# Hybrid decoder layer on one core: the first row norm stepped beside its output projection, convolution taps as single chains in one PSUM bank, the convolution norm in a bank of its own, and squares added on GpSimd

## The chip, the core and the metric

The kernel runs on one core of one Trainium2 chip, as one launch. The metric is device microseconds (us) for one execution of the program. The core has a matrix engine (TensorE, PE; its weight loads are listed apart as PEld), a vector engine (VectorE, DVE), a scalar engine (ScalarE, ACT), GpSimd (POOL), a sync engine (SyncE, SP) that issues loads, and DMA queues. Each engine works through its own list of instructions in a fixed order; an instruction waits until the work that it needs on other engines has signalled.

## The reference

One decoder layer over x of 1024 tokens by 1024 channels, in float32, cut to what matters here:

```
proj = x @ w_in + b_in                    # 1024 x 1792
q, k, v, a, gate = split(proj)            # 512, 128, 128, 512, 512
# attention group: window of 128, 8 heads of 64, 2 kv heads, a sink logit per head, relative bias
y_attn = sliding_window_gqa(q, k, v, sinks, rel_bias_table)
# convolution group
h = a * sigmoid(gate)
h = causal_depthwise_conv(h, conv_dw_w, conv_dw_b)        # 31 taps per channel
y_conv = silu(layer_norm(h, conv_ln_g, conv_ln_b))        # over the 512 channels
y = concat(rms_norm(y_attn, attn_out_gain), rms_norm(y_conv, conv_out_gain))
x = layer_norm(ALPHA * x + y @ w_out + b_out, ln1_g, ln1_b)
# feed-forward
hh = causal_depthwise_conv(x @ w_up, ffn_dw_w, ffn_dw_b)  # 3 taps, 5632 channels
g, u = split(hh)
x = layer_norm(ALPHA * x + (silu(g) * u) @ w_down, ln2_g, ln2_b)
```

## The kernel before

**Halves and products.** The 1024 tokens are worked in two halves, H = 0 and H = 1, of 512 tokens each. A 512-token row of one 128-channel group is one tile of 128 x 512. A float32 product is made as three products of fp32r parts: each operand is split into a high part (`wh`, `oh`: a cast on ACT, L231) and a low part (`wl`, `ol`: a subtraction on POOL, L233), and TensorE multiplies high by high, high by low and low by high (`mm3`, L265, L266, L268).

**Stages.** For each half there are input projections (`load_x`, `glu`, `proj_kv`, `proj_q`), the 31-tap convolution (`conv`), its norm (`conv_norm`), attention (`attn`: per 128-token block and pair of heads a `front`, scores and softmax; a `mid`, the transposes L541; a `back`, the products with v, L562 to L564; and per block a `tail`, L581), the output projection (`out_proj`: 16 tiles of 128 x 2 x 256, four quarters of the columns `q` by four token blocks `t`, each added into `acc` by two DVE instructions, L652 and L654), the first row norm (`ln1`, which also transposes the normed rows into the feed-forward's operand, L278 and L282) and the feed-forward. Six of 22 channel pairs of the feed-forward are done for half 0 alone (`ffn`, up products by `mm3`, then down products); the other 16 are done for both halves together (`joint`), by seven products in place of eight. This joint loop is the last half of the run.

**The convolution.** Of 31 taps, the first KO (4 for half 0, 5 for half 1) are done as ACT multiplications (L411) added on POOL (L415); the rest, 27 and 26 of them, are a chain of DVE instructions (L421 for the first, L425 for the others), each of which reads the running sum in PSUM and writes it again, until the last writes the result tile `cy`. POOL then adds its own sum (L430). `conv_pair` works two channel groups at a time and alternates between their two chains, each in one of the two banks with the tag C.

**The convolution norm.** The mean over the 512 channels is a product with a constant matrix of 1/512 (L445). Then `y[c] - mean` on DVE (L449), a square on ACT (L451), and for each of four token blocks the sum of squares over the 512 channels as four matmuls with one column (L456, output 128 x 1). After 1/sqrt (DVE L292, POOL L293) the four columns are made into a row by a product with a diagonal matrix (L462, L464), and the rows are scaled, gated and split (L469 to L472). The same sums of squares for the RMS norm follow (L480). All these PSUM tiles have the tag C too. A float32 matmul shows as two records in the trace.

**What sets the order.** `SCRIPT` is a string of letters; each letter advances one generator by one step: `a`/`A` attention of half 0/1, `c`/`C` convolution, `n`/`N` convolution norm, `g` and `q` the projections of half 1, `o`/`O` output projection of half 0/1, `l`/`L` first row norm, `f` feed-forward of half 0. In the kernel before, `c` and `C` run their generator to its end at once. That gives the order in which the instructions are written. The framework's scheduler then sets the final order on each engine by a timeline of its own, under the data dependencies, the PSUM tiles that must come free, and two chains of order that the kernel adds: `chain` keeps the bulk products (`mm3`, the output projection of half 0, the joint products) in the order written, and `tap` does the same for the convolution's DVE taps, over both halves. DMA loads keep their order as well.

**PSUM.** Eight banks are dealt out by tag: `PS` gives A 2, S 2, T 1, Y 1, C 2. `PT` says which tags a stage cycles through: the row norm of half 0 (`ln0`) uses A, that of half 1 (`ln1`) T and C, the joint products A, T, S, A, C, S, Y, C.

Of the kernel before, what the change touches and what calls it, by code (L numbers as in the profile page):

```python
# [15 lines left out]
P = 128  # L16
S = 1024
# [16 lines left out]
LINE = 384  # L34
GROUP = 2
ALONE = 6
SCRIPT = ('0hx00j0hxixxiiiacaaaaaaaaaaaaannnaaagaggqqgaaaqkqoAAAoAAAAAo'
          'ACAoAAllAANAAAANAlAlfNfAOOOfsOsssffLLLLffff')
SKEW = (1, 2, 5)
KOFF = (4, 5)  # L40
AHEAD = 1
LNM = (0, 0, 1, 1)
XM = (1, 1)
PT = {'x0': 'AT', 'x1': 'AS', 'glu0': 'AS', 'glu1': 'A', 'kv0': 'A', 'kv1': 'A', 'q0': 'A', 'q1': 'A', 'v0': 'T', 'v1': 'T',
      'joint': 'ATSACSYC',
      'tail': 'T', 'out0': 'A', 'out1': 'A', 'ln0': 'A', 'ln1': 'TC', 'sum1': 'T', 'up0': 'A', 'up1': 'AY', 'down0': 'SY', 'down1': 'S'}
PS = {'A': 2, 'S': 2, 'T': 1, 'Y': 1, 'C': 2}
UNIT = 512
BASE = 384
D0 = 74  # L50
# [19 lines left out]
def hybrid_layer_kernel(  # L70
# [153 lines left out]
    def cdw(k, c):  # L224
        return pcol(1, k * 4 + c)
# [175 lines left out]
            nc.gpsimd.tensor_tensor(out=ql[:, i, :], in0=qf, in1=f(qh[:, i, :]), op=ALU.subtract)  # L401
            yield

    def conv_pair(H, c0, dst):
        KO = KOFF[H]
        extra = {}
        for i, c in enumerate((c0, c0 + 1)):
            for k in range(KO):
                slot = 2 * i if k == 0 else 1
                prod = at(64 * 4 * UNIT + 4 * (HC + slot * HALF), [P, HALF], F32, "cp")  # L410
                nc.scalar.mul(out=prod, in_=hconv[H, c][:, k:k + HALF], mul=cdw(k, c))  # L411
                if k == 0:
                    extra[c] = prod
                else:
                    nc.gpsimd.tensor_tensor(out=extra[c], in0=extra[c], in1=prod, op=ALU.add)  # L415
        chains = {c: psB(tag="C") for c in (c0, c0 + 1)}
        for k in range(KW - 1, KO - 1, -1):
            for c in (c0, c0 + 1):
                src = hconv[H, c][:, k:k + HALF]
                if k == KW - 1:  # L420
                    tap(nc.vector.tensor_scalar(out=chains[c], in0=src, scalar1=cdw(k, c), scalar2=cdb[c],  # L421
                                                op0=ALU.mult, op1=ALU.add))
                else:
                    to = dst[c] if k == KO else chains[c]
                    tap(nc.vector.scalar_tensor_tensor(out=to, in0=src, scalar=cdw(k, c), in1=chains[c],  # L425
                                                       op0=ALU.mult, op1=ALU.add))
            if k % 8 == 0:
                yield
        for c in (c0, c0 + 1):
            nc.gpsimd.tensor_tensor(out=dst[c], in0=dst[c], in1=extra[c], op=ALU.add)  # L430

    def conv(H):
        y = [sbt([P, HALF], "cy") for c in range(4)]
        for c0 in (0, 2):
            yield from conv_pair(H, c0, y)
        cyt[H] = y

    def conv_norm(H):
        y = cyt[H]
        mean = psB(tag="C")  # L440
        sums = [sbt([P, HALF], "nsum") for _ in range(2)]
        for i in range(2):
            nc.gpsimd.tensor_tensor(out=sums[i], in0=y[2 * i], in1=y[2 * i + 1], op=ALU.add)
        nc.gpsimd.tensor_tensor(out=sums[0], in0=sums[0], in1=sums[1], op=ALU.add)
        nc.tensor.matmul(out=mean, lhsT=ones, rhs=sums[0], start=True, stop=True)  # L445
        var = psB((P, 4), "C")
        sqs = []
        for c in range(4):
            nc.vector.tensor_tensor(out=y[c], in0=y[c], in1=mean, op=ALU.subtract)  # L449
            sq = sbt([P, HALF], "nsq")  # L450
            nc.scalar.square(out=sq, in_=y[c])  # L451
            sqs.append(sq)
        yield
        for t in range(TB):
            for c in range(4):
                nc.tensor.matmul(out=var[:, t:t + 1], lhsT=sqs[c][:, t * P:(t + 1) * P], rhs=ones[:, 0:1],  # L456
                                 start=c == 0, stop=c == 3)
        rstd = ring("crstd", 4, 2)
        rsqrt_eps(rstd, var, 4, "nrv")
        dg = sbt([P, TB, P], "nz")  # L460
        for t in range(TB):
            nc.vector.tensor_scalar(out=dg[:, t, :], in0=ident, scalar1=rstd[:, t:t + 1], scalar2=None, op0=ALU.mult)  # L462
        rb = psB(tag="C")
        nc.tensor.matmul(out=rb, lhsT=ones1, rhs=dg, start=True, stop=True)  # L464
        yield
        yh, yl = [[a[:, c, :] for c in range(4)] for a in pair(1)]
        sqs = []
        for c in range(4):
            nc.vector.tensor_tensor(out=y[c], in0=y[c], in1=rb, op=ALU.mult)  # L469
            nc.scalar.activation(out=y[c], in_=y[c], func=AF.Silu, bias=clb[c], scale=clg[c])  # L470
            nc.scalar.mul(out=yh[c], in_=y[c], mul=gain[4 + c])
            nc.vector.scalar_tensor_tensor(out=yl[c], in0=y[c], scalar=gain[4 + c], in1=f(yh[c]),  # L472
                                           op0=ALU.mult, op1=ALU.subtract)
            sq = sbt([P, HALF], "nsq")
            nc.scalar.square(out=sq, in_=y[c])
            sqs.append(sq)
        ms = psB((P, 4), "C")
        for t in range(TB):
            for c in range(4):
                nc.tensor.matmul(out=ms[:, t:t + 1], lhsT=sqs[c][:, t * P:(t + 1) * P], rhs=ones[:, 0:1],  # L480
                                 start=c == 0, stop=c == 3)
        s = ring("sC", 4, 2)
        rsqrt_eps(s, ms, 4, "nrv")
        yC[H] = (yh, yl)
        sC[H] = s
        yield

    def attn(H):
# [59 lines left out]
        def back(u):  # L548
# [16 lines left out]
            if (g, pr) == (1, 1):  # L565
                yh, yl = [a[:, :, t * P:(t + 1) * P] for a in qT[H]]
                yv = yp[t].rearrange("p (i q) -> p i q", q=P)
                for i in range(4):
                    nc.scalar.mul(out=yh[:, i], in_=yv[:, i], mul=gain[i])
                for i in range(4):  # L570
                    nc.vector.scalar_tensor_tensor(out=yl[:, i], in0=yv[:, i], scalar=gain[i], in1=f(yh[:, i]),
                                                   op0=ALU.mult, op1=ALU.subtract)
                sq = sbt([P, HALF], "sq")
                nc.scalar.square(out=sq, in_=yp[t])
                sqs[t] = sq
                yA[b] = (yh, yl)

        def tail(t):
            ms = psk("tail", (P, 4))
            for i in range(4):  # L580
                nc.tensor.matmul(out=ms[:, 0:1], lhsT=sqs[t][:, i * P:(i + 1) * P], rhs=ones[:, 0:1],  # L581
                                 start=i == 0, stop=i == 3)
            rsqrt_eps(s[:, t:t + 1], ms[:, 0:1], 1)

        n = len(units)
# [425 lines left out]
    drain(load_x(0))  # L1011
    parameters()
    for k in SCRIPT:
        if k in 'cC':
            drain(steps[k])
        else:
            next(steps[k], None)
# [60 lines left out]
```

## Time and profile before

| what | value |
|---|---|
| median of 3 runs | 1140.39 us (1139.77 to 1141.25) |
| the profiled execution | 1140.95 us, of which the span in the trace is 1139.2 us |
| busy in the span | PE 95%, PEld 79%, DVE 68%, ACT 46%, POOL 53% |
| mean granted clock of TensorE | 0.967 |
| projections of both halves begun, 0 to 120 us | PE busy 111.1 of 120 |
| attention and conv norm of half 0, projections of half 1, 120 to 233 us | PE busy 113.0 of 113, clock 0.92 |
| output projection of half 0 beside conv and attention of half 1, 233 to 317 us | DVE busy 81.1 of 84 |
| row norm of half 0, conv norm and attention of half 1, 317 to 364 us | PE busy 37.2 of 47, clock 0.75 |
| feed-forward of half 0 begun, 364 to 399 us | PE busy 34.7 of 35, clock 0.84 |
| output projection and row norm of half 1, feed-forward of half 0, 399 to 547 us | PE busy 138.7 of 148 |
| joint loop, end, 547 to 1139.2 us | PE busy 574.4 of 592.2 |

How to read the lines that follow: a row of the timeline gives start and length in us, the engine, the line of the kernel, the instruction, its output and inputs, and how many instructions were merged into the row ("x22"); in brackets stands the idle time of the engine before it and what ended it. A group row gives busy time in us and the mean length in ns, then the idle time before the group. The granted clock (PEclk) is the share of full speed that TensorE was given; 0.50 is half speed. Instructions of one engine overlap a little, so the step from one start to the next is the better price of a row of equal instructions than the length of each.

### The profile page before, as it was taken

To read this page: it belongs to the slowest core of one execution; us is meant where nothing else is said; L and a number is where in the kernel's file an instruction comes from. 1 tells how busy PE (TensorE), PEld (TensorE's weight loads), DVE (VectorE), ACT (ScalarE), POOL (GpSimd) and SP (SyncE) were. 2 spreads that over 40 slices of the span, in tenths; PEclk is the share of its full clock that TensorE was granted. 3 is DMA by queue.
4 is the path that set the end of the run, shared out by engine and by line. 5 is a ranking of instruction groups with operands and counts; after the bars stand their busy time and mean duration, and the time that the engine had idled before them with its cause. 6 is when DMAs were issued, how large, how long until landed. Compare 5 with 4: busy or idle time off the path is not lost.

```text
span 1139.2 us, 14637 instructions
## 1 busy us (share of the span) xinstructions
PE 1084.8 (95%) x5257; PEld 903.9 (79%) x5257; DVE 776.6 (68%) x1414; ACT 521.3 (46%) x1031; POOL 599.1 (53%) x468
## 2 busy tenths in 40 slices
PE   7999999998888999989999999999999999999997
PEld 5877788888876899867778787878878787888875
DVE  3699555999996355998565747474656656559656
ACT  4536897673659432444424334251524242442530
POOL 4739645446461165834837465564636373835561
PEclk9999988999968899999999999999999999999998
DMA  5534212233220034113211112121212021223421
GB/s 179 167 97 116 72 32 66 83 93 119 67 93 19 1 121 120 57 38 92 73 38 56 56 38 75 37 75 37 65 28 75 19 75 37 70 99 115 125 93 74
DMA packets 115642, 85.21 MB, mean 75 GB/s; under 512 B 20354, under 2 KB 108017, under 8 KB 115569
## 3 DMA queue, kind: packets, MB, share of 16 engines
q1 hardware_dynamic: 112368, 78.92, 23.2%
q10 hardware_dynamic: 3201, 5.35, 1.3%
q8 instruction: 41, 0.67, 0.2%
q14 instruction: 32, 0.26, 0.1%
HBM read 80.05 MB, written 4.21 MB: 74 GB/s over the span
## 4 chain that ended last, share of the span: by engine, by line
PE 45%; DVE 5%; ACT 1%; DMA 0%; POOL 0%; issue 0%; POOLq 0%; ACTq 0%
PE psC L800 2%; PE psC L798 2%; PE psC L797 2%; PE psS L800 2%; PE psS L797 2%; PE psS L798 2%; PE psA L800 2%; PE psA L798 2%; PE psA L797 2%; PE psS L717 2%; PE psS L718 2%; PE psS L719 2%; PE psA L717 1%; PE psC L717 1%; PE psA L718 1%; PE psA L719 1%
## 5 line engine op out<-in xcount | busy, mean ns | idle before, releaser
L233 POOL TENSOR_TENSOR wl<-raw,wh 128x512 fp32r<-128x512 f32 x196 | 263.0, 1354 | 223.4 <-PE psA L268 86.3
L231 ACT CAST wh<-raw 128x512 fp32r<-128x512 f32 x196 | 118.7, 619 | 172.0 <-PE psA L266 19.2
L233 POOL TENSOR_TENSOR wl<-ts,wh 128x512 fp32r<-128x512 f32 x64 | 82.5, 1296 | 149.6 <-ACT wh L231 136.5
L265 PE MATMUL psA<-x,wh 128*128 128x512 f32 x336 | 138.2, 411 | 7.9 <-DVE z L682 3.5
L266 PE MATMUL psA<-x,wh 128*128 128x512 f32 x336 | 137.4, 409 | 0.0
L425 DVE SCALAR_TENSOR_TENSOR psC<-hconv,const,psC 128x512 f32<-128x512 f32 x196 | 135.8, 742 | 0.0
L231 ACT CAST wh<-ts 128x512 fp32r<-128x512 f32 x64 | 39.4, 622 | 174.4 <-PE psS L719 31.0
L268 PE MATMUL psA<-x,wl 128*128 128x512 f32 x336 | 90.6, 404 | 0.6 <-POOL wl L233 0.6
L265 PEld LDWEIGHTS psA<-x,wh 128*128 128x128 f32 x336 | 66.1, 197 | 24.0 <-issue 4.4
L266 PEld LDWEIGHTS psA<-x,wh 128*128 128x128 f32 x336 | 66.0, 197 | 14.6 <-issue 0.7
L268 PEld LDWEIGHTS psA<-x,wl 128*128 128x128 f32 x336 | 63.9, 193 | 15.8 <-issue 1.2
L293 POOL TENSOR_TENSOR tiny<-tiny,const 128x1 f32<-128x1 f32 (+1 forms) x28 | 27.6, 989 | 61.3 <-DVE tiny L292 61.3
L233 POOL TENSOR_TENSOR ol<-or,oh 128x512 fp32r<-128x512 f32 x32 | 41.0, 1307 | 26.8 <-PE psY L564 15.4
L724 DVE TENSOR_TENSOR acc<-psS,acc 128x512 f32<-128x512 f32 x52 | 35.6, 687 | 26.9 <-PE psS L719 26.9
L797 PE MATMUL psS<-x,wh 128*128 128x512 f32 x112 | 43.6, 389 | 0.0
L797 PE MATMUL psA<-x,wh 128*128 128x512 f32 x112 | 43.6, 389 | 0.0
L798 PE MATMUL psA<-x,wh 128*128 128x512 f32 x112 | 43.6, 389 | 0.0
L798 PE MATMUL psS<-x,wh 128*128 128x512 f32 x112 | 43.6, 389 | 0.0
L797 PE MATMUL psC<-x,wh 128*128 128x512 f32 x112 | 43.6, 389 | 0.0
L798 PE MATMUL psC<-x,wh 128*128 128x512 f32 x112 | 43.6, 389 | 0.0
L415 POOL TENSOR_TENSOR cp<-cp,cp 128x512 f32<-128x512 f32 x28 | 36.0, 1286 | 13.0 <-ACT cp L411 13.0
L836 POOL TENSOR_TENSOR ts<-raw,ts 128x512 f32<-128x512 f32 x32 | 41.6, 1299 | 1.2
(340 smaller groups left out, 3084.3 us busy)
## 6 DMA issues: line engine op xcount, KB each, us to landing
raw<-in_w_up SPq DMA_DIRECT2D x56, 512.0 KB
raw<-in_w_down SPq DMA_DIRECT2D x28, 512.0 KB
raw<-in_w_in SPq DMA_DIRECT2D x20, 512.0 KB
raw<-in_x SPq DMA_DIRECT2D x8, 512.0 KB
raw<-in_w_in SPq DMA_DIRECT2D x16, 256.0 KB
acc<-in_x SPq DMA_DIRECT2D x8, 512.0 KB
or<-in_w_out SPq DMA_DIRECT2D x64, 64.0 KB
or<-in_w_out SPq DMA_DIRECT2D x8, 512.0 KB
```

Of the source, the lines that this page charges most:

```text
L231: nc.scalar.copy(out=h, in_=part)
L233: nc.gpsimd.tensor_tensor(out=l, in0=part, in1=f(h), op=ALU.subtract)
L265: m.append(nc.tensor.matmul(out=o, lhsT=wh[kt], rhs=xh[kt], start=kt == 0, stop=False))
L266: m.append(nc.tensor.matmul(out=o, lhsT=wh[kt], rhs=xl[kt], start=False, stop=False))
L268: m.append(nc.tensor.matmul(out=o, lhsT=wl[kt], rhs=xh[kt], start=False, stop=kt == KT - 1))
L415: nc.gpsimd.tensor_tensor(out=extra[c], in0=extra[c], in1=prod, op=ALU.add)
L425: tap(nc.vector.scalar_tensor_tensor(out=to, in0=src, scalar=cdw(k, c), in1=chains[c], op0=ALU.mult, op1=ALU.add))
L717: m.append(nc.tensor.matmul(out=o, lhsT=gh[:, tsl], rhs=wh, start=j == 0, stop=False))
L797: m.append(nc.tensor.matmul(out=o, lhsT=wh[k], rhs=xh[k], start=k == 0, stop=False))
L798: m.append(nc.tensor.matmul(out=o, lhsT=wh[k], rhs=xl[k], start=False, stop=False))
L800: m.append(nc.tensor.matmul(out=o, lhsT=wl[k], rhs=xh[k], start=False, stop=k == 3))
L836: nc.gpsimd.tensor_tensor(out=t, in0=x0, in1=x1, op=ALU.subtract)
```

## The change

`SCRIPT` steps the convolution of half 1 one channel group at a time, between steps of the output projection and attention, and puts four steps of the row norm of half 0 (`l`) right after the last step of its output projection. `conv_pair` becomes `conv_group`: one channel group is one chain of 27 or 26 taps, in the only bank C. The bank that this frees gets a tag of its own, N, for all tiles of `conv_norm`; the joint products use N where they had their second C, and the row norm of half 1 cycles through T, C and N. `token_sums` adds the four tiles of squares into one on POOL (three additions of 128 x 512) and then needs one matmul with one column for each token block in place of four. In attention's `tail` the squares, 512 wide, are folded by POOL to 256 and to 128, and one matmul takes the place of four.

```
-SCRIPT = ('0hx00j0hxixxiiiacaaaaaaaaaaaaannnaaagaggqqgaaaqkqoAAAoAAAAAo'
-          'ACAoAAllAANAAAANAlAlfNfAOOOfsOsssffLLLLffff')
+SCRIPT = ('0hx00j0hxixxiiiacaaaaaaaaaaaaannnaaagaggqqgaaaqkqoAAAoAAAAA'
+          'oACCCCAoAllllAANAAAANAAfNfAAOOOfsOsssffLLLLffff')
...
-      'joint': 'ATSACSYC',
-      'tail': 'T', 'out0': 'A', 'out1': 'A', 'ln0': 'A', 'ln1': 'TC', 'sum1': 'T', ...
-PS = {'A': 2, 'S': 2, 'T': 1, 'Y': 1, 'C': 2}
+      'joint': 'ATSACSYN',
+      'tail': 'T', 'out0': 'A', 'out1': 'A', 'ln0': 'A', 'ln1': 'TCN', 'sum1': 'T', ...
+PS = {'A': 2, 'S': 2, 'T': 1, 'Y': 1, 'C': 1, 'N': 1}
...
+    def conv_group(H, c, dst):
+        KO = KOFF[H]
+        for k in range(KO):
...
+        total = psB(tag="C")
         for k in range(KW - 1, KO - 1, -1):
+            src = hconv[H, c][:, k:k + HALF]
+            if k == KW - 1:
+                tap(nc.vector.tensor_scalar(out=total, in0=src, scalar1=cdw(k, c), scalar2=cdb[c],
+                                            op0=ALU.mult, op1=ALU.add))
+            else:
+                tap(nc.vector.scalar_tensor_tensor(out=dst if k == KO else total, in0=src, scalar=cdw(k, c),
+                                                   in1=total, op0=ALU.mult, op1=ALU.add))
+        nc.gpsimd.tensor_tensor(out=dst, in0=dst, in1=extra, op=ALU.add)
...
+    def token_sums(o, sqs):
+        for a, b in ((0, 1), (2, 3), (0, 2)):
+            nc.gpsimd.tensor_tensor(out=sqs[a], in0=sqs[a], in1=sqs[b], op=ALU.add)
+        for t in range(TB):
+            nc.tensor.matmul(out=o[:, t:t + 1], lhsT=sqs[0][:, t * P:(t + 1) * P], rhs=ones[:, 0:1],
+                             start=True, stop=True)
...
     def conv_norm(H):
-        mean = psB(tag="C")
+        mean = psB(tag="N")
...
-        for t in range(TB):
-            for c in range(4):
-                nc.tensor.matmul(out=var[:, t:t + 1], lhsT=sqs[c][:, t * P:(t + 1) * P], rhs=ones[:, 0:1],
-                                 start=c == 0, stop=c == 3)
+        token_sums(var, sqs)
...
+                for w in (2 * P, P):
+                    nc.gpsimd.tensor_tensor(out=sq[:, 0:w], in0=sq[:, 0:w], in1=sq[:, w:2 * w], op=ALU.add)
...
-            for i in range(4):
-                nc.tensor.matmul(out=ms[:, 0:1], lhsT=sqs[t][:, i * P:(i + 1) * P], rhs=ones[:, 0:1],
-                                 start=i == 0, stop=i == 3)
+            nc.tensor.matmul(out=ms[:, 0:1], lhsT=sqs[t][:, 0:P], rhs=ones[:, 0:1], start=True, stop=True)
...
-        if k in 'cC':
+        if k == 'c':
             drain(steps[k])
```

Three places show how the instructions move. The first is DVE around the first taps of half 1's convolution. Before, the first tap of all (L421, its source is the half's tile `hconv_1553`) stands among the last instructions of half 0's conv norm (L469 scales, L472 splits; between them two instructions of attention):

```order
L469 TENSOR_TENSOR cy_780<-cy_780,psC 128x512
L516 ISA hank_258,tiny_60<-psS,bias_577,const_61 128x256
L516 ISA tiny_60 128x1
L516 ISA hank_258,tiny_60<-psS,bias_577,const_61 128x256
L516 ISA tiny_60 128x1
L544 TENSOR_TENSOR ph_948<-psT,ph_948 128x512
L472 SCALAR_TENSOR_TENSOR x_93<-cy_777,const_61,x_92 128x512
L472 SCALAR_TENSOR_TENSOR x_93<-cy_778,const_61,x_92 128x512
L421 TENSOR_SCALAR psC<-hconv_1553,const_61 128x512
```

In the changed kernel the last tap of half 0 (to `cy_780`) is followed by the taps of half 1 (L418 and L421 now; source `hconv_1532`), which stand ahead of all instructions of half 0's conv norm:

```order
L421 SCALAR_TENSOR_TENSOR cy_780<-hconv_238,const_61,psC 128x512
L538 TENSOR_TENSOR ph_967<-psT,ph_967 128x256
L418 TENSOR_SCALAR psC<-hconv_1532,const_61 128x512
L521 TENSOR_TENSOR tiny_60<-tiny_60 128x4
L421 SCALAR_TENSOR_TENSOR psC<-hconv_1532,const_61,psC 128x512
L522 RECIPROCAL tiny_60<-tiny_60 128x4
L421 SCALAR_TENSOR_TENSOR psC<-hconv_1532,const_61,psC 128x512 x3
```

So the taps of half 1 have moved from behind the conv norm of half 0 to directly behind the last tap of half 0, and three of them in a row now belong to the same chain, each reading what the one before wrote.

The second place is PE at the conv norm of half 1, beside the transposes of half 0's row norm (L278). Before, sixteen matmuls of one column are in the list (four tiles of squares, `nsq`, for each token block); these are the last eight, with one token block's transposes between them:

```order
L456 MATMUL psC<-const_61,nsq_3165 128x1
L456 MATMUL psC<-const_61,nsq_3168 128x1
L456 MATMUL psC<-const_61,nsq_3171 128x1
L456 MATMUL psC<-const_61,nsq_3174 128x1
L456 MATMUL psC<-const_61,nsq_3165 128x1
L278 MATMUL psA<-const_61,acc_1998 128x128 x8
L456 MATMUL psC<-const_61,nsq_3168 128x1
L456 MATMUL psC<-const_61,nsq_3171 128x1
L456 MATMUL psC<-const_61,nsq_3174 128x1
```

In the changed kernel the same place has the mean (L445), the attention's tail (L576) and four matmuls of one column (L435) between the transposes of the first three token blocks:

```order
L445 MATMUL psN<-nsum_3138,const_61 128x512
L278 MATMUL psA<-const_61,acc_1976 128x128 x8
L576 MATMUL psT<-const_61,sq_1061 128x1
L278 MATMUL psA<-const_61,acc_1979 128x128 x8
L435 MATMUL psN<-const_61,nsq_3146 128x1 x4
L535 MATMUL psT<-const_61,hank_254 128x128 x4
L278 MATMUL psA<-const_61,acc_1982 128x128 x8
```

The number of such matmuls is a quarter, and transposes that stood behind them stand ahead of them.

The third place is POOL near the end of half 0's output projection. Before, the last two splits of its weights (`ol`) are followed by the additions to the convolution's last two results (L430 to `cy_2658`, `cy_2659`):

```order
L233 TENSOR_TENSOR wl_282<-raw_166,wh_284 128x512
L233 TENSOR_TENSOR wl_170<-raw_201,wh_168 128x512
L233 TENSOR_TENSOR ol_2031<-or_2027,oh_2029 128x512
L233 TENSOR_TENSOR ol_2035<-or_2027,oh_2033 128x512
L443 TENSOR_TENSOR nsum_3157<-cy_2656,cy_2657 128x512
L430 TENSOR_TENSOR cy_2658<-cy_2658,cp_781 128x512
```

In the changed kernel that addition (L423 now, to the last result `cy_2636`) stands ahead of those two splits:

```order
L423 TENSOR_TENSOR cy_2636<-cy_2636,cp_819 128x512
L233 TENSOR_TENSOR wl_282<-raw_166,wh_284 128x512
L233 TENSOR_TENSOR wl_170<-raw_201,wh_168 128x512
L233 TENSOR_TENSOR ol_2009<-or_2005,oh_2007 128x512
L233 TENSOR_TENSOR ol_2013<-or_2005,oh_2011 128x512
L570 TENSOR_TENSOR sq_1061<-sq_1061 128x256
L570 TENSOR_TENSOR sq_1061<-sq_1061 128x128
```

The last weights of the output projection are now split behind the end of the convolution, not ahead of it. The order of loads on SP is the same, load for load.

More of the change, by code (lines that the diff above doesn't have):

```diff
@@ L44 @@
 PT = {'x0': 'AT', 'x1': 'AS', 'glu0': 'AS', 'glu1': 'A', 'kv0': 'A', 'kv1': 'A', 'q0': 'A', 'q1': 'A', 'v0': 'T', 'v1': 'T',
-      'joint': 'ATSACSYC',
-      'tail': 'T', 'out0': 'A', 'out1': 'A', 'ln0': 'A', 'ln1': 'TC', 'sum1': 'T', 'up0': 'A', 'up1': 'AY', 'down0': 'SY', 'down1': 'S'}
-PS = {'A': 2, 'S': 2, 'T': 1, 'Y': 1, 'C': 2}
+      'joint': 'ATSACSYN',
+      'tail': 'T', 'out0': 'A', 'out1': 'A', 'ln0': 'A', 'ln1': 'TCN', 'sum1': 'T', 'up0': 'A', 'up1': 'AY', 'down0': 'SY', 'down1': 'S'}
+PS = {'A': 2, 'S': 2, 'T': 1, 'Y': 1, 'C': 1, 'N': 1}
 UNIT = 512
@@ L402, in proj_q @@
             yield
-    def conv_pair(H, c0, dst):
+    def conv_group(H, c, dst):
         KO = KOFF[H]
[L406 to L416, printed above, removed]
-        for k in range(KW - 1, KO - 1, -1):
[L418 to L430, printed above, removed]
@@ L432, in conv @@
-    def conv(H):
[L433 to L436, printed above, removed]
+        for k in range(KO):
+            slot = 2 * (c % 2) if k == 0 else 1
+            prod = at(64 * 4 * UNIT + 4 * (HC + slot * HALF), [P, HALF], F32, "cp")
+            nc.scalar.mul(out=prod, in_=hconv[H, c][:, k:k + HALF], mul=cdw(k, c))
+            if k == 0:
+                extra = prod
+            else:
+                nc.gpsimd.tensor_tensor(out=extra, in0=extra, in1=prod, op=ALU.add)
@@ new lines, in conv_group @@
+        total = psB(tag="C")
+        for k in range(KW - 1, KO - 1, -1):
+            src = hconv[H, c][:, k:k + HALF]
+            if k == KW - 1:
+                tap(nc.vector.tensor_scalar(out=total, in0=src, scalar1=cdw(k, c), scalar2=cdb[c],
+                                            op0=ALU.mult, op1=ALU.add))
+            else:
+                tap(nc.vector.scalar_tensor_tensor(out=dst if k == KO else total, in0=src, scalar=cdw(k, c),
+                                                   in1=total, op0=ALU.mult, op1=ALU.add))
@@ new lines, in conv_group @@
+        nc.gpsimd.tensor_tensor(out=dst, in0=dst, in1=extra, op=ALU.add)
+    def conv(H):
+        cyt[H] = [sbt([P, HALF], "cy") for c in range(4)]
+        for c in range(4):
+            conv_group(H, c, cyt[H][c])
+            yield
+    def token_sums(o, sqs):
[4 more added lines that the diff above has]
+                             start=True, stop=True)
@@ L445, in conv_norm @@
         nc.tensor.matmul(out=mean, lhsT=ones, rhs=sums[0], start=True, stop=True)
-        var = psB((P, 4), "C")
+        var = psB((P, 4), "N")
         sqs = []
@@ L462, in conv_norm @@
             nc.vector.tensor_scalar(out=dg[:, t, :], in0=ident, scalar1=rstd[:, t:t + 1], scalar2=None, op0=ALU.mult)
-        rb = psB(tag="C")
+        rb = psB(tag="N")
         nc.tensor.matmul(out=rb, lhsT=ones1, rhs=dg, start=True, stop=True)
@@ L476, in conv_norm @@
             sqs.append(sq)
[L477 to L481, printed above, removed]
+        ms = psB((P, 4), "N")
+        token_sums(ms, sqs)
         s = ring("sC", 4, 2)
```

## The prediction, made before the changed kernel was run

> **What bounds the kernel now.** I read the page's head and clock row first, then busy time by stage, then the timeline at the edges of the stages that the change touches. The page: PE is busy 95% of the span and the whole run leans on it, but its clock dips in the second quarter, where DVE is at its fullest.
>
> ```profile
> span 1139.2 us, 14637 instructions
> PE 1084.8 (95%) x5257; PEld 903.9 (79%) x5257; DVE 776.6 (68%) x1414; ACT 521.3 (46%) x1031; POOL 599.1 (53%) x468
> DVE  3699555999996355998565747474656656559656
> PEclk9999988999968899999999999999999999999998
> ```
>
> By stage (stretch; then length and the busy time with count of PE, PEld, DVE, ACT, POOL; granted clock; DMA share; GB/s):
>
> ```profile
> 120.00:233.00 113.00, 113.00 (x564) 92.85 (x562) 74.36 (x163) 88.78 (x208) 54.60 (x46) 0.92 0.23 64
> 233.00:317.00 84.00, 75.70 (x545) 70.17 (x544) 81.11 (x188) 46.88 (x133) 46.71 (x40) 0.94 0.33 101
> 317.00:364.00 47.00, 37.24 (x179) 31.03 (x178) 39.47 (x79) 33.72 (x75) 16.87 (x9) 0.75 0.14 48
> 364.00:399.00 35.00, 34.67 (x167) 29.48 (x168) 12.94 (x28) 18.74 (x42) 6.61 (x6) 0.84 0.00 0
> 547.00:1139.20 592.20, 574.37 (x2523) 472.60 (x2522) 373.26 (x615) 212.46 (x358) 315.58 (x244) 0.99 0.21 65
> ```
>
> So four stages before 399 us have different limits. Up to 233 it is PE, partly at a low clock. In the output projection of half 0 it is DVE: 81.1 of 84 us. In the row norm it is nobody's throughput: PE stands 10 of 47 us and runs at a clock of 0.75, while DVE works off the row norm, the convolution norm and attention in one list. Then PE again. The last row, more than half of the run, is PE alone; it is the same work in the changed kernel, so what is gained or lost ahead of it is passed on whole. The edges of the DVE-bound stretch are the first and the last addition of the projection, and the row norm ends where TensorE gets its operand:
>
> ```profile
> 242.75 0.45 DVE L652 SCALAR_TENSOR_TENSOR acc<-psA,tiny,acc 128x256 f32<-128x256 f32 x1
> 316.38 0.47 DVE L654 SCALAR_TENSOR_TENSOR acc<-psA,tiny,acc 128x256 f32<-128x256 f32 x1
> 356.45 0.50 PE L265 MATMUL psA<-x,wh 128*128 128x512 f32 x1 [0.88 <-DVE x L282]
> ```
>
> **Part 1: fewer matmuls of one column.** Groups (busy us, mean ns) and two runs of them:
>
> ```profile
> L456 PE MATMUL psC<-const,nsq x64: 164/352/372, 150.0 to 337.0; 128*128 128x1 f32 x64
> L480 PE MATMUL psC<-const,nsq x64: 164/250/352, 177.7 to 380.5; 128*128 128x1 f32 x64
> L581 PE MATMUL psT<-const,sq x64: 164/250/371, 185.3 to 406.7; 128*128 128x1 f32 x64
> 329.58 4.94 PE L456 MATMUL psC<-const,nsq 128*128 128x1 f32 x22 [0.35 <-ACT nsq L451]
> 377.08 2.62 PE L480 MATMUL psC<-const,nsq 128*128 128x1 f32 x20
> 150.87 0.97 PE L511 MATMUL psS<-kh,x 64*128 64x256 f32 x6
> ```
>
> 192 records (two to a matmul) become 48. A record costs 2.62 / 20 = 0.131 us at mostly full clock and 4.94 / 22 = 0.225 at the low one. Ahead of the first matmul of the output projection the written order has 40 such matmuls before and 10 now, 60 records less, 7.9 us; one more group of scores (0.97 us) has moved ahead of it. Net -6.9 us on the path, as PE is busy all of 113 us there. After the first `mm3` of the feed-forward it is again 30 matmuls less, 7.9 us by the same price, of which I count 4 (a run as long as the row norm's now stands ahead of that point, and the POOL work below must come first).
>
> **Part 2: the clock.** Rows: stretch, then PE, PEld, DVE, ACT and POOL as above, clock.
>
> ```profile
> 374.00:377.00 3.00, 3.00 (x24) 2.81 (x23) 0.95 (x4) 1.75 (x2) 1.28 (x1) 1.00 0.00 0
> 377.00:381.00 4.00, 4.00 (x30) 4.00 (x29) 2.80 (x7) 3.30 (x9) 0.55 (x1) 0.73 0.01 4
> 381.00:385.00 4.00, 4.00 (x10) 3.13 (x11) 1.02 (x3) 0.77 (x2) 1.02 (x1) 0.50 0.00 0
> 153.00:157.00 4.00, 4.00 (x24) 4.00 (x23) 2.73 (x8) 4.00 (x11) 1.35 (x2) 0.57 0.32 64
> 157.00:164.00 7.00, 7.00 (x22) 5.42 (x22) 2.56 (x10) 5.58 (x15) 2.31 (x2) 0.51 0.00 0
> ```
>
> The clock falls from 1.00 to 0.50 during and after a run of these matmuls in which PE is never idle. The stretch 120 to 233 loses 113 x 0.08 = 9.0 us to it, 364 to 399 loses 35 x 0.16 = 5.6. With runs of 8 records in place of 32, between none and all of this comes back: 0 to 14.6. I take half of the first, -4.5, and 3 of the second. The Trainium skill, "TensorE: Matmul & The Clock Gate", section "Why this matters for your kernels", ties the drop to a PE-idle gap of about 3 us. The rows above show a drop with no gap; by that rule these drops have another cause and nothing of the 7.5 comes back (rival A).
>
> **Part 3: taps as one chain.** Rows of DVE: a run of alternating taps, then a dependent pair (L808 reads the z that L806 wrote) and an independent neighbour:
>
> ```profile
> 54.88 13.91 DVE L425 SCALAR_TENSOR_TENSOR psC<-hconv,const,psC 128x512 f32<-128x512 f32 x21
> 578.25 0.74 DVE L806 SCALAR_TENSOR_TENSOR z<-psA,const,z 128x511 f32<-128x511 f32 x1
> 579.02 0.75 DVE L808 SCALAR_TENSOR_TENSOR z<-psA,const,z 128x510 f32<-128x510 f32 x1
> 579.69 0.74 DVE L806 SCALAR_TENSOR_TENSOR sq<-psC,const,sq 128x511 f32<-128x511 f32 x1
> ```
>
> A tap steps 13.91 / 21 = 0.66 us. The dependent pair steps 0.77, the independent one 0.67: +0.10, and I take 0.125 as the dearest step that I saw of this kind. No row shows a PSUM chain of taps back to back: the cost is 0 if the tap's write is ready in its own step, 0.125 by the pair. In the changed order 103 of 212 taps follow directly on a tap of their own chain, 62 in half 0 and 41 in half 1: +7.8 and +5.1 us of DVE. The first part lies where DVE is 90% busy or more (57 to 114 us) but PE is the bound; it delays half 0's conv norm, whose result is due only at the output projection, near 233 (its first addition is at 242.75). What is late next if this cover goes is the conv norm's mean, for which PE would stand. I count +1. The second part falls where DVE idles (part 4): 0.
>
> **Part 4: half 1's taps start early.** Now they stand behind the conv norm, because it holds the banks C:
>
> ```profile
> 127.00:174.00 47.00, 21.28 (x61) 0.89 0.20 49
> 174.23 0.81 DVE L421 TENSOR_SCALAR psC<-hconv,const 128x512 f32<-128x512 f32 x1
> 174.00:191.00 17.00, 7.04 (x20) 0.90 0.18 54
> 191.06 0.81 DVE L421 TENSOR_SCALAR psC<-hconv,const 128x512 f32<-128x512 f32 x1
> ```
>
> (The two stretches are of DVE alone.) DVE idles 25.7 and 10.0 us there; room for 23 taps at 0.66 + 0.125 = 18 us. In the written order 153 taps stand ahead of the first addition of the output projection before, 176 now: 23 x 0.66 = 15.2 us less in the DVE-bound stretch. Into it come the four `acc` scalings of half 1 (L627), 4 x 1.21 = 4.8:
>
> ```profile
> 330.24 1.21 DVE L627 SCALAR_TENSOR_TENSOR acc<-acc,bo 128x1024 f32<-128x1024 f32 x1
> L415 POOL TENSOR_TENSOR cp<-cp,cp 128x512 f32<-128x512 f32 x28 | 36.0, 1286 | 13.0 <-ACT cp L411 13.0
> ```
>
> Net -10.4. On POOL the last two `ol` splits now stand behind the addition to the last convolution tile, L423: five instructions of about 1.29 (L415's row) are 6.4 us after the last tap, while eleven additions are still to come; I charge +2, between 0 and 6.4.
>
> **Part 5: the row norm.** DVE is busy 39.5 of the 47 us here, in a list in which row norm, convolution norm and attention wait for each other: a stretch of 47 / 39.5 = 1.19. The four scalings leave the list, 4.8 us: 34.7 x 1.19 = 41.3, so -5.7. The transposes of three blocks now stand ahead of the convolution norm's sums, which by itself lets the feed-forward begin sooner. Against it, `token_sums` puts three POOL additions into the convolution norm's chain: 3.9 us at 1.29 each, 7.1 at 2.35 (L444, below). The 32 records that they replace took 7.2 at 0.225. Bounds: 0 (what leaves the list turns into waiting) and -12.3 (the list runs dense, 34.7). I take -6, the middle.
>
> **POOL as a whole** gets 12 additions (15.4 us) and 16 folds; a fold of 256 or 128 columns is not in the trace, so between 0.3 (L415 by width) and 1.29, I take 0.9: 14 us. POOL is busy 53%, so this is hidden behind its idle time except in part 5's chain. The squares of attention have one buffer, `sq`: ACT's square for the next block waits for both folds, 1.8 us, and for the one matmul, where it waited for eight records (1.0 to 1.8 us by the two prices). Behind it in ACT's list stand the casts and exponentials of the next units; 0 to +1 per block, and 0 taken, since ACT has 37 of 84 us free. SP's loads keep their order and cost nothing. The row norm of half 1 gets a third bank: between 0 and -4 (a wait for a bank), I take 0.
>
> **Sum.** -6.9 - 4 - 4.5 - 3 + 1 - 10.4 + 2 - 6 = -31.8. Not all of a DVE saving is seen by PE, which itself works 75.7 of the 84 us of that stretch: its room is 8.3, so I count -8.3 in place of -10.4 + 2, and a quarter off the rest (23.4) for waits that come late next, ACT's softmax and the `ph` copies in front: -8.3 - 17.6 = -26. From the profiled 1140.95 us: 1115; the median of the runs, 1140.39, lies 0.6 below, so I say 1115 for it too.
>
> **Rivals.** A: the low clock stays. Then 7.5 of the sum stays lost, and the row norm keeps its 0.75: -26 + 7.5 + 2 = -16.5, 1124. For it: the clock is at its lowest, 0.75, in the stage in which PE stands most. Against: the rows of part 2. The rule of the page named there speaks for it. B: dependent taps and the new POOL links eat the gain: DVE +12.9 on the path, tails +2 and L423 6.4 in full: -26 + 12.9 - 1 + 2 + 6.4 = -5.7, about 1135; with the low clock too, no change. For it: DVE is the bound for 84 us; against: most of the self-waits are outside that stretch. C, slower: POOL's additions hold DVE up. Rows:
>
> ```profile
> 315.66 0.79 DVE L311 TENSOR_SCALAR acc<-acc,tiny 128x1024 f32<-128x1024 f32 x1
> 319.12 2.93 DVE L311 TENSOR_SCALAR acc<-acc,tiny 128x1024 f32<-128x1024 f32 x1
> 319.15 2.35 POOL L312 TENSOR_TENSOR acc<-acc,g 128x1024 f32<-128x1024 f32 x1
> 316.84 2.35 POOL L444 TENSOR_TENSOR nsum<-nsum,nsum 128x512 f32<-128x512 f32 x1
> ```
>
> L311 alone takes 0.79 us, beside a POOL instruction 2.93: 2.14 lost in 2.35. If all 29 us of new POOL work did that to DVE where DVE is on the path, +26.5, it would undo the whole sum; from 26 / 29 = 0.9 us lost per us on it decides. That is 1142, and 1145 if the three additions of the norm also take 2.35 each. Against it: the run of 21 taps at 0.66 lies beside L415 on POOL. The Trainium skill, "GPSIMD Engine Reference", section "8. Key points", says that GpSimd shares SBUF interfaces with VectorE and collides with DVE instructions in a two-port mode or with two SBUF inputs; a tap and an addition of the projection take one input from PSUM, and the row of taps agrees; L311 goes through 1024 columns in 0.79 us where a tap needs 0.66 for 512, and it is the one that is held up. D: better, all low-clock stretches go and the row norm shrinks to its list: 1115 - 7.5 - 5 = 1102.
>
> **Numbers.** My forecast, 1108 to 1120: 0.45. A, 1120 to 1130: 0.22. B, 1130 to 1143: 0.13, of which a third within 0.2% (2.3 us, about what this measurement can tell from no change). C: 0.10. D, below 1108: 0.10. So faster 0.84, same 0.05, slower 0.11. The range leaves out half of D and all of C and the end of B: 1100 to 1135.
>
> **What would show it.** Right: the clock of 150 to 200 us near 1.00; DVE busy in 127 to 190 with taps; the first addition of the projection near 233, the last near 297; the first `mm3` of the feed-forward near 333; the joint loop unchanged in length. A shows as clock rows of 0.5 after the POOL additions; B as taps stepping 0.78 between additions with PE waiting for DVE, or PE waiting for `ol`; C as DVE instructions of the norms at two to four times their lengths. I am wrong if attention's softmax, which shares DVE and ACT, already sets the pace of the row norm: then only the first 233 us gain.

## The result, and the profile after

The changed kernel takes 1124.93 us (median of 4 runs, 1122.67 to 1127.36), the kernel before 1140.82 us (4 runs, 1139.77 to 1141.91): a ratio of 0.9873, 95% interval 0.9848 to 0.9898. That is 15.9 us faster, where 26 were forecast. The time lies inside the range of 1100 to 1135 us, but above the band of my forecast, 1108 to 1120, and in the band of rival A, 1120 to 1130. The working behind it was right in some terms and wrong in others.

The page of the changed kernel, its head, DVE and clock rows:

```profile
span 1125.6 us, 14364 instructions
PE 1055.0 (94%) x5113; PEld 876.9 (78%) x5113; DVE 788.1 (70%) x1414; ACT 520.7 (46%) x1031; POOL 623.6 (55%) x496
DVE  2898898999895438994756656574747566569656
PEclk9999999999978999998999999999999999999999
```

PE is busy 30 us less, DVE 11.5 us more (788.1 against 776.6). DVE's three slices at 5 tenths before (114 to 199 us) now read 8, 9 and 8. By stretch (columns as before the change):

```profile
120.00:233.00 113.00, 104.81 (x534) 84.50 (x533) 102.31 (x210) 98.11 (x227) 78.97 (x68) 0.95 0.25 71
233.00:317.00 84.00, 74.39 (x554) 69.11 (x552) 78.11 (x174) 46.87 (x136) 43.57 (x36) 0.96 0.37 113
317.00:364.00 47.00, 34.36 (x168) 28.66 (x169) 32.58 (x72) 38.84 (x82) 22.81 (x20) 0.82 0.04 12
547.00:1125.60 578.60, 558.74 (x2441) 459.27 (x2439) 361.18 (x597) 203.64 (x344) 300.83 (x232) 0.99 0.21 65
```

In 120 to 233 us DVE does 27.9 us more than before and POOL 24.4 more, and PE, which never stopped there, now stands 8.2 us. The edges of the stages, from the timeline of DVE and PE: first and last addition of half 0's output projection (L646, L648), first `mm3` of the feed-forward (L265), first matmul of half 1's output projection (L636):

```profile
239.09 0.48 DVE L646 SCALAR_TENSOR_TENSOR acc<-psA,tiny,acc 128x256 f32<-128x256 f32 x1 [0.48 <-PE psA L642]
308.17 0.47 DVE L648 SCALAR_TENSOR_TENSOR acc<-psA,tiny,acc 128x256 f32<-128x256 f32 x1
344.51 0.80 PE L265 MATMUL psA<-x,wh 128*128 128x512 f32 x1 [4.67 <-ACT x L281]
376.33 0.39 PE L636 MATMUL psA<-oh,x 128*128 128x256 f32 x1 [0.59 <-ACT oh L231]
```

The same matmul of half 1 before:

```profile
398.42 0.39 PE L642 MATMUL psA<-oh,x 128*128 128x256 f32 x1
```

So the gain stands at 3.7 us at the first addition, 8.2 at the last, 11.9 at the feed-forward's first matmul and 22.1 at half 1's output projection; the span then ends only 13.6 us sooner (1139.2 - 1125.6). In this one execution 8.5 us are given back after 376 us.

### The profile page after: what moved, and what is told of

It reads as the page before. It is cut to its first block, busy times and chain, and to the rows that moved or that the text cites. A ratio compares the mean times of both kernels' runs of the same rounds, so it can differ in the third digit from the quotient of the medians.

```text
span 1125.6 us, 14364 instructions
## 1 busy us (share of the span) xinstructions
PE 1055.0 (94%) x5113; PEld 876.9 (78%) x5113; DVE 788.1 (70%) x1414; ACT 520.7 (46%) x1031; POOL 623.6 (55%) x496
## 3 DMA queue, kind: packets, MB, share of 16 engines
q1 hardware_dynamic: 112368, 78.92, 23.5%
## 4 chain that ended last, share of the span: by engine, by line
PE 74%; DVE 13%; ACT 5%; POOL 3%; DMA 3%; issue 1%; POOLq 0%; SPq 0%; DVEq 0%; ACTq 0%
PE psA L265 5%; PE psA L266 5%; PE psA L268 5%; PE psS L711 3%; PE psS L712 2%; PE psS L713 2%; PE psS L794 2%; PE psA L794 2%; PE psA L791 2%; PE psS L791 2%; PE psS L792 2%; PE psA L792 2%; PE psS L505 1%; PE psA L711 1%; PE psA L712 1%; PE psA L713 1%
## 5 line engine op out<-in xcount | busy, mean ns | idle before, releaser
L233 POOL TENSOR_TENSOR wl<-raw,wh 128x512 fp32r<-128x512 f32 x196 | 263.5, 1354 | 171.6 <-ACT wh L231 75.9
L233 POOL TENSOR_TENSOR wl<-ts,wh 128x512 fp32r<-128x512 f32 x64 | 82.5, 1296 | 157.2 <-ACT wh L231 136.1
L265 PE MATMUL psA<-x,wh 128*128 128x512 f32 x336 | 138.1, 411 | 15.2 <-ACT x L281 4.7
L421 DVE SCALAR_TENSOR_TENSOR psC<-hconv,const,psC 128x512 f32<-128x512 f32 x196 | 147.4, 752 | 3.3
L265 PEld LDWEIGHTS psA<-x,wh 128*128 128x128 f32 x336 | 66.1, 197 | 31.7 <-issue 5.0
L233 POOL TENSOR_TENSOR ol<-or,oh 128x512 fp32r<-128x512 f32 x32 | 41.3, 1311 | 38.1 <-ACT oh L231 24.4
L293 POOL TENSOR_TENSOR tiny<-tiny,const 128x1 f32<-128x1 f32 (+1 forms) x28 | 23.4, 837 | 48.8 <-DVE tiny L292 48.8
L711 PE MATMUL psS<-wh,gh 128*128 128x512 f32 x88 | 35.6, 404 | 7.3 <-ACT gh L815 3.8
L636 PE MATMUL psA<-oh,x 128*128 128x256 f32 x128 | 38.0, 297 | 1.6 <-DVE acc L648 1.0
```

The costliest lines, as they stand in the source:

```text
L233: nc.gpsimd.tensor_tensor(out=l, in0=part, in1=f(h), op=ALU.subtract)
L265: m.append(nc.tensor.matmul(out=o, lhsT=wh[kt], rhs=xh[kt], start=kt == 0, stop=False))
L421: tap(nc.vector.scalar_tensor_tensor(out=dst if k == KO else total, in0=src, scalar=cdw(k, c), in1=total, op0=ALU.mult, op1=ALU.add))
L636: m.append(nc.tensor.matmul(out=pa[:, 0, :], lhsT=yah[:, c, :], rhs=wa[0][c], start=c == 0, stop=False))
L711: m.append(nc.tensor.matmul(out=o, lhsT=gh[:, tsl], rhs=wh, start=j == 0, stop=False))
```

## Experiments

All ratios are to runs of the kernel before on the same chip. There the kernel before spread more (1132 to 1143 us), so the intervals are wide, 0.25 to 0.5% to each side; I compare kernels by ratios and call a difference shown only where intervals are apart or a trace shows the place.

| kernel | median us | ratio, 95% interval |
|---|---|---|
| changed kernel, again | 1123.53 | 0.9880 (0.9828 to 0.9931) |
| old_sums | 1125.42 | 0.9902 (0.9871 to 0.9934) |
| sums_only | 1130.34 | 0.9932 (0.9899 to 0.9965) |
| pair0 | 1127.99 | 0.9925 (0.9899 to 0.9952) |
| norm_early_only | 1141.61 | 1.0029 (1.0003 to 1.0054) |
| norm_later | 1119.10 | 0.9841 (0.9796 to 0.9885) |
| shared_bank | 1133.27 | 0.9963 (0.9939 to 0.9987) |
| var1_mm | 1124.33 | 0.9884 (0.9840 to 0.9929) |
| taps_only | 1123.91 | 0.9879 (0.9835 to 0.9923) |
| later_tc | 1116.55 | 0.9817 (0.9785 to 0.9849) |
| later_var1_tc | 1117.17 | 0.9821 (0.9790 to 0.9852) |
| half_taps | 1110.11 | 0.9761 (0.9716 to 0.9805) |

**The changed kernel again.**

> The changed kernel once more, for a second trace. In the first trace half 1's output projection began 22 us sooner than before, but the end came only 13.6 us sooner; 3.1 us of that went in one wait inside the joint loop (TensorE for ACT's gh at 689 us). If that is a chance event, this trace has seven equal groups of 61.3 us in the joint loop and the time is 1122 to 1125; if it belongs to the changed order, one group has 64.4 us again and the time is 1124 to 1128.

1123.53 us, a time in the range of the chance event, but the trace has the longer group of the joint loop again: 63.9 us, the others 61.3 (the first, which holds other work, apart). So it belongs to this program. POOL waits there for a weight load:

```profile
680.64 1.29 POOL L830 TENSOR_TENSOR ts<-raw,raw 128x512 f32<-128x512 f32 x1 [3.33 <-DMA raw<-in_w_up]
```

In old_sums, whose group has 61.2 us, the same wait is

```profile
677.46 1.29 POOL L829 TENSOR_TENSOR ts<-raw,raw 128x512 f32<-128x512 f32 x1 [1.11 <-DMA raw<-in_w_up]
```

The other groups of the changed kernel wait 1.2 to 1.5 us there. The late load is not of this program alone: pair0, norm_later, shared_bank, half_taps and later_tc have it in the same group, with waits of 2.6 to 2.8 us, and old_sums has it one group earlier, 2.81 us. Nor has it one price: that group is longer by 2.4 to 2.7 us in the first four, by 0.9 in later_tc and 1.0 in old_sums. What made the load late is open.

**Undo the squares on POOL** (sixteen and four matmuls of one column again):

```
-        token_sums(var, sqs)          # and ms; attention's folds go too
+        for t in range(TB):
+            for c in range(4):
+                nc.tensor.matmul(out=var[:, t:t + 1], lhsT=sqs[c][...], rhs=ones[:, 0:1], ...)
```

> The changed kernel, but with four matmuls of one column per token block again, in the norm and in attention's tail, and no additions of squares on POOL. Theory (fewer such matmuls free TensorE and keep its clock up): the 12 us of matmuls come back on the path and low-clock stretches return after them near 160 and 190 us, 1136 to 1143. Rival (the additions on POOL cost as much in the norm's chain as they save): 1122 to 1128.

1125.42: no loss that can be told. The rows say where the matmuls' time went. First matmul and last addition of half 0's output projection:

```profile
236.45 0.28 PE L635 MATMUL psA<-oh,x 128*128 128x256 f32 x1
309.59 0.47 DVE L647 SCALAR_TENSOR_TENSOR acc<-psA,tiny,acc 128x256 f32<-128x256 f32 x1
```

The projection begins at 236.5 where the changed kernel begins at 229.6 (227.3 in its second trace): the matmuls do cost about 7 us. It ends at 309.6 against 308.2 (305.7): most of it is lost again. The expected 12 us on the path fell. The theory's other half came true: low-clock stretches return, here at 171 and 202 us (rows under part 2), but PE stands only 3.8 us in 120 to 233, where the changed kernel has 8.2.

**The squares on POOL alone**, on the kernel before:

> The kernel before with only the additions of squares on POOL. Theory: fewer matmuls bring 10 to 16 us by themselves, 1125 to 1131, with a clock near 1.00 between 150 and 190 us. Rival: without the earlier taps the output projection of half 0 stays bound by DVE at 74 us and the row norm waits for the same list, so no more than the 7 us ahead of it are kept, 1133 to 1140.

1130.34, 8 us better than its kernel before (ratio 0.9932): the time is within the theory's range, the gain short of its 10 to 16 us. The clock of 150 to 190 us is 1.00, as expected. Its last addition comes at 320.5, later than before (316.4), and still the whole is faster: what was won is won in the row norm's stretch, not ahead of the projection.

**Alternating chains for half 0**, in banks C and N:

```
+        if H == 0:
+            for c0 in (0, 2):
+                yield from conv_pair(H, c0, cyt[H])   # chains = psB(tag="CN"[c - c0])
+            return
```

> The changed kernel, but half 0's convolution works two channel groups with alternating chains again, in the banks C and N (N is free until half 0's norm); half 1 keeps single chains. Theory: the single chains cost 0.13 us per tap and end half 0's convolution 9.8 us later, which puts its norm's ACT work beside half 1's convolution products and makes TensorE wait 6 us near 190 us and then run 7 us at half clock; with alternating chains these waits go and the output projection begins 5 to 9 us sooner, 1116 to 1121. Rival: ACT's list is as full without that delay, 1123 to 1126.

1127.99: not faster, perhaps slower. My theory fell. The last tap of half 0 is at 127.8 us (140.6 in the changed kernel, 127.0 before), but the wait near 190 us did not go: PE now stands there for DVE, in whose list taps of half 1 lie between attention's steps, and the clock of 190 to 203 us is 0.74 (0.61 and 0.74 in the changed kernel's two traces).

```profile
190.63 1.65 PE L537 MATMUL psS<-kh,x 64*128 64x256 f32 x6 [3.53 <-DVE tiny L542]
```

The projection's first matmul is at 225.6, 4.0 and 1.8 us sooner than in those two traces, not 5 to 9. The last addition is at 309.2 all the same:

```profile
309.21 0.43 DVE L680 SCALAR_TENSOR_TENSOR acc<-psA,tiny,acc 128x256 f32<-128x256 f32 x1
```

**The row norm's place alone**, on the kernel before, and **the row norm at its old place**, on the changed kernel:

```
-          'ACAoAAllAANAAAANAlAlfNfAOOO...'          -  'oACCCCAoAllllAANAAAANAAfNfAAOOO...'
+          'ACAoAllllAANAAAANAAfNfAAOOO...'          +  'oACCCCAoAAllAANAAAANAlAlfNfAOOO...'
```

> The kernel before with only the row norm's four steps put right after the last step of half 0's output projection (alternating chains, shared banks, sixteen matmuls as before). Theory (the row norm waits for DVE's list, and that list holds 59 taps beside the output projection in any case): 2 to 6 us better than before. Rival (the place of the row norm alone brings what was seen at half 1's output projection, 22 us): 10 us or more better than before.

> The changed kernel with the row norm's steps at their old places in the script. Theory (DVE's shorter list lets the row norm begin, wherever it is written): 3 to 8 us slower than the changed kernel. Rival (the place is what matters): 10 us or more slower than the changed kernel, near the kernel before.

1141.61, slightly slower than before, and 1119.10, not slower than the changed kernel; both expectations of a gain fell. The row norm's early steps bring nothing. In norm_later half 1's output projection begins at 371.9 us, sooner than with them.

**The norm in the banks C**, shared:

```
-PS = {..., 'C': 1, 'N': 1}        # and tag="N" in conv_norm, 'TCN', 'ATSACSYN'
+PS = {..., 'C': 2}
```

> The changed kernel with the two banks C shared by the single chains and the convolution norm, as before, and no bank N. Theory (the bank of its own lets half 1's taps start 50 us sooner, which takes 23 taps out of the DVE-bound stretch): taps of half 1 start after half 0's norm again, more than 50 of them stand in the stretch, and the time is 6 to 12 us over the changed kernel's. Rival (a single chain needs only one of two banks, so it finds one free as early): within 3 us of the changed kernel.

1133.27, about 9.5 us over the changed kernel, intervals apart: the theory's size. First tap of half 1, last addition, half 1's mean, and the longest of the waits in its output projection:

```profile
198.54 0.80 DVE L418 TENSOR_SCALAR psC<-hconv,const 128x512 f32<-128x512 f32 x1
305.14 0.47 DVE L648 SCALAR_TENSOR_TENSOR acc<-psA,tiny,acc 128x256 f32<-128x256 f32 x1
360.13 1.02 PE L445 MATMUL psC<-nsum,const 128*128 128x512 f32 x2
378.48 1.86 PE L435 MATMUL psC<-const,nsq 128*128 128x1 f32 x8 [7.13 <-POOL nsq L433]
```

The taps do start after half 0's norm, at 198.5 (141.9 in the changed kernel, below), and 45 of them, not the more than 50 expected, stand between the first and the last addition, where it has 36. But the last addition is no later, 305.1. The loss comes behind it: half 1's convolution ends at 354.7 us, its norm begins at 360 (311.5 in the changed kernel), and half 1's output projection, begun at 364.9, waits for that norm and ends its additions at 453.6, where the changed kernel ends them at 440.0. So the bank is worth its 10 us through half 1's norm, not through the additions of half 0.

**Half of half 1's taps left out**, to see what sets the end of the projection:

```
+            if H == 1 and KO < k < KW - 1 and k % 2 == 0:
+                continue
```

> The changed kernel without 12 of the 26 DVE taps of each channel group of half 1 (they are left out, so the result is another). That takes 48 taps, 32 to 38 us of DVE, out of the work ahead of the last addition of half 0's output projection. Theory (DVE's list sets the end of that stretch): the last addition comes at 285 us or earlier, where the changed kernel has 306 to 308. Rival (the stretch is set by TensorE and by attention's chain through ACT, and DVE's taps only fill it): it stays at 300 or later, and the whole gains less than 8 us.

The last addition moves from 306 to 308 us to 300.5 only, though some 34 us of DVE work are gone, and DVE idles 23.5 us between first and last addition. The windows row of that stretch, and DVE's longest wait in it (total, times, longest):

```profile
227.80:301.00 73.20, 70.78 (x555) 67.01 (x554) 44.53 (x127) 43.51 (x130) 37.22 (x33) 1.00 0.43 139
DVE acc L648 <- PE psA L644: 13.1, 8, 4.5
```

PE is busy 70.8 of 73.2 us at full clock: with DVE out of the way it is PE that sets the end. The theory that DVE alone does fell at once. The rival's second half (less than 8 us in all) fell too: the whole gains 13, since the row norm behind it runs sooner (first `mm3` at 331.8).

**Part of the sums undone.** Only half 1's first sums of squares are matmuls again:

> The changed kernel, but half 1's first sums of squares, those inside the row norm's stretch, are again sixteen matmuls; all other sums stay on POOL. With all sums by matmul the feed-forward began at 339 us where the changed kernel has 342 to 344, and then lost 7 us to 28 records. Theory (POOL's three additions lengthen the chain of the convolution norm just where DVE and the row norm wait for it): the feed-forward begins 3 to 5 us sooner and the whole is 3 to 5 us faster than the changed kernel, 1118 to 1121. Rival (the order moved by chance): within 2 us of the changed kernel or slower.

1124.33: within the changed kernel's interval, the rival's case.

**The chains and the bank alone** (old_sums with the row norm at its old place):

> The single chains and the bank N alone: the changed kernel with sixteen matmuls again and with the row norm's steps at their old places. Shared banks cost the changed kernel about 10 us, POOL's sums alone brought 8 to the kernel before, the early row norm brought nothing or lost 4. If the parts add, this is 1138 - 10 = 1126 to 1130. Theory (sums and bank work on the same wait, half 1's convolution norm, so the bank alone brings nearly all): 1118 to 1124.

1123.91, the theory's upper end, and as fast as the changed kernel: chains and bank by themselves bring all that the change brings; on top of them POOL's sums, which alone brought 8 us, and the row norm's place add nothing that can be told. This run also keeps the convolution of half 1 stepped between the projection's steps; that step was not tried apart from the chains.

**Without the third bank of half 1's row norm**, row norm at its old place:

```
-      'ln1': 'TCN'
+      'ln1': 'TC'
```

> The changed kernel with the row norm's steps at their old places and half 1's row norm back on the banks T and C. In the first traces half 1's row norm to the first joint product took 67.3 us with the third bank, 65.5 before. Theory (the third bank brings nothing, it costs 2 us by taking N from the convolution norm's place in the order): 65 to 66 us there, 1116 to 1118. Rival: it makes no difference, 1118 to 1121.

> The row norm's steps at their old places, banks T and C for half 1's row norm, and sixteen matmuls for the first sums of squares of half 1; the rest as in the changed kernel. If each of the three edits keeps what it showed, 1114 to 1118, the fastest so far; if they are one and the same wait, 1117 to 1121.

1116.55 and 1117.17. later_tc has the lowest median of those that compute the whole layer: its interval ends at 0.9849, where that of the changed kernel begins at 0.9848 (first timing) and 0.9828 (second), so it is at the edge of what can be told. Against norm_later (0.9841) the intervals overlap. Its trace takes 66.3 us from half 1's last addition to the first joint product, norm_later 67.2, the changed kernel 67.3: 1 us, not the 2 expected. Here too one joint group is longer, but by 0.9 us.

## Why the prediction was right in sign and short in size

**Part 1, fewer matmuls.** The price was right: 6.9 us ahead of the output projection forecast, 6.9 to 9.1 between old_sums and the changed kernel's two traces. What failed is counting it as path: the last addition comes only 1.4 to 3.9 us sooner.

**Part 2, the clock.** Loss in 120 to 233 us: 113 x 0.05 = 5.6 us, before 9.0, so 3.4 came back, not the 4.5 taken. In 364 to 399 us the clock reads 0.95, before 0.84: 3.9 us where 3 was taken, though by now other work stands in that window. The stretch of 150 to 164 us now runs at full clock. But a new low stretch starts at 191, and it starts in a wait:

```profile
189.67 0.97 PE L505 MATMUL psS<-kh,x 64*128 64x256 f32 x6 [0.43 <-DVE tiny L510]
194.58 0.58 PE L556 MATMUL psY<-ph,vpad 128*128 128x256 f32 x1 [3.93 <-ACT ph L537]
197.26 0.80 PE L265 MATMUL psA<-x,wh 128*128 128x512 f32 x1 [2.10 <-ACT z L351]
```

The page of the Trainium skill that I set against the trace ("TensorE: Matmul & The Clock Gate", "Why this matters for your kernels") fits this one: 3.93 us of standing, then matmuls at half speed. The moment fits less well: the granted clock falls 1.2 us into the standing here, and just behind 3.95 us of it in the second trace. The rule does not fit the drop of before at 153 us, which had no gap. Nor does it fit old_sums, where that drop moved together with the long run of one-column matmuls, again without a gap (the two stretches are of PE alone):

```profile
166.97 2.39 PE L434 MATMUL psN<-const,nsq 128*128 128x1 f32 x20
167.00:171.00 4.00, 4.00 (x33) 1.00 0.19 59
171.00:178.00 7.00, 7.00 (x25) 0.53 0.00 0
```

So what I took to drive this term holds: in the four traces with 192 records (before, norm_early_only, old_sums, taps_only) each of the eight long runs of half 0's norm, 22 to 34 records, has a low stretch that starts 1 to 5 us after the run does. In the other traces, whose runs there have 8 records, the clock fell within 5 us of a run only once, in sums_only at 194 us, and there PE had stood 2.29 us. Why a busy PE drops its clock in such a run is not shown.

**Part 3, single chains.** The step per tap was sized right, its effect placed wrong. Taps in a row:

```profile
59.40 10.26 DVE L421 SCALAR_TENSOR_TENSOR psC<-hconv,const,psC 128x512 f32<-128x512 f32 x13
```

10.26 / 13 = 0.79 us, +0.13 over 0.66 (0.125 forecast). The last tap of half 0 came 13.6 us later, not 7.8, and I had counted +1 for that: 73 of the 103 dependent taps lie in half 0, not 62, which is 9.5 us, and the first tap comes 2.8 us later (32.3, before 29.5). What it pushed is ACT's list near 190 us: half 0's norm now falls there (its mean is at 154.0, before 143.2) beside the products of half 1's convolution, and attention's cast L537, for which PE waits 3.93 us, stands behind them:

```profile
191.69 0.72 ACT L468 ACTIVATE x<-cy,const 128x512 fp32r<-128x512 f32 x1
192.31 0.61 ACT L472 ACTIVATE nsq<-cy 128x512 f32<-128x512 f32 x1
192.83 0.60 ACT L231 CAST wh<-raw 128x512 fp32r<-128x512 f32 x1
193.34 0.72 ACT L409 ACTIVATE cp<-hconv,const 128x512 f32<-128x512 f32 x1
193.96 0.56 ACT L537 CAST ph<-psT 128x512 fp32r<-128x512 f32 x1
```

The first addition gained 3.7 us (5.9 in the second trace) in place of 10.4. How much of the shortfall is the chains' doing stays open. sums_only, with the old chains and banks, gained no more than 5.9 there, for in it PE stands too, 3.7 of the 106 us from 120 on, where it never stood before: once its own list is shorter, PE waits for ACT, DVE and POOL. And pair0 only put another wait in this one's place.

**Part 4, half 1's taps start early.** They do:

```profile
141.86 0.81 DVE L418 TENSOR_SCALAR psC<-hconv,const 128x512 f32<-128x512 f32 x1
```

From first to last addition there are 36 taps in place of 59, 15.7 us less, and four scalings more, 4.9; the forecast had 15.2 and 4.8. The stretch shrank by 4.5 us, not 8.3: attention instructions moved into it, and DVE idles 4.9 us in it (2.9 before). Here is the step that failed most: I added the earlier start and the shorter stretch. They are not a sum: 16.1 us forecast for both (10.4 less a quarter, and 8.3), 8.2 measured. The last addition comes between 305 and 310 us with 28, 30, 36 and 45 taps in the stretch (old_sums, pair0, changed kernel, shared_bank) and with starts 11 us apart; half_taps shows PE's own matmuls as the next limit, 300.5.

**Part 5, the row norm.** From the last addition to half 1's output projection 68.2 us, before 82.0: -13.9, the place where the change pays most (-13 forecast for it, with 4 and 3 from parts 1 and 2, -9.8 after my cut by a quarter). In its parts it fits less: 3.7 us up to the feed-forward's first matmul, where 6 were taken for the row norm, and 10.1 behind it, where 7 were, so that the sum fits is in part luck. One of the reasons given was not a cause: norm_later has 66.8 us from the last addition to half 1's projection without the row norm's early steps. The scalings did leave DVE's list, as forecast, but the forecast had no term for what stands beside them: half 1's convolution now ends ahead of this stretch (last tap at 280.5, before 312.3), so its norm begins at 311.5 in place of 320.0. DVE is busy 32.6 us of the 47 from 317 us on, before 39.5; 34.7 were forecast. shared_bank shows the same from the other side: norm at 360, and the gain is lost.

**The rest,** counted at 0, cost 8.5 us in the first trace: 3.1 in the joint loop's one group, 1.5 in half 1's output projection, 1.8 in its row norm with three banks, 2.1 after the joint loop (norm_early_only, with the old chains, has this last one too). The second trace gives back 8.1 in all. later_tc gives back 0.3 (741.02 us from half 1's first projection matmul to the end, before 740.75). Of this only the group with the late load is placed; why the other edits remove the rest is open.

**POOL.** The added work was sized well (12 x 1.44, 8 x 0.95 and 8 x 0.46 = 28.5 us; 29 forecast), and rival C, POOL holding DVE up, did not come: DVE is busy 11.5 us longer in all, less than the 103 x 0.13 = 13.4 us of the dependent taps. (Beside the prediction's run of 21 taps stand L233 and L369 on POOL, not L415; they are 128x512 instructions of 1.28 us all the same.) Rival A's 1124 is the measured time, but not by its mechanism: of the low clock 3.4 and 3.9 us did come back, 7.3 of the 7.5 taken.

## To carry to other kernels

A gain ahead of a stretch and a gain inside it add only if the same engine sets both; find the next limit of the stretch first (here, in the 69 us from first to last addition, PE's 63 us of matmuls beside DVE's 64) and take the gain against that. A buffer of its own for a chain that runs beside others can be worth more than the instructions saved: what counted was that half 1's convolution and norm no longer queued behind the rest. When several edits go in together, run each alone and each undone: here one of three was enough for the whole gain, the second brought half of it alone and nothing beside the first, and the third brought nothing.

## What the hardware showed that was not expected

A DVE tap that reads the PSUM tile written by the tap just ahead steps 0.79 us, an alternating one 0.66: 99 of 103 such pairs lie between 0.75 and 0.82, none lower. A run of 22 or more records of one-column matmuls went with a fall of the granted clock to 0.51 to 0.57 while PE stood in no gap: 153 to 164 us before, 171 to 178 in old_sums, 168 to 178 in taps_only. In the joint loop POOL waits about 1 us or more for the weights in nearly every group, so a late load finds no slack on POOL: waits of 2.6 to 3.3 us went with a group 0.9 to 3.1 us longer. The kernel before spreads over 1132 to 1143 us on one chip with one program; which stretch makes the difference was not traced.
